# Half of the down product of an MLP as seven block products in place of eight, with the first sum of weight blocks on GpSimd

## The chip, the cores and the metric

One core of one Trainium2 chip runs the kernel. The metric is the device time of one execution in microseconds (us); the median of three runs of the kernel before is 2241.0 us (2240.79 to 2241.18). Engines are named as in the profile: PE multiplies matrices, DVE is VectorE, ACT is ScalarE, POOL is GpSimd, SP issues the DMAs.

## The reference

A decoder trunk of two layers on 256 tokens of 2048 features in float32. Each layer is a mixer (attention of several kinds) and then a dense MLP with a hidden width of 8192; a last norm follows. The part that matters here:

```python
def squared_relu_mlp(h, w1, w2):
    return jnp.square(jax.nn.relu(h @ w1)) @ w2

for layer in range(DEPTH):
    x = x + mixer(rmsnorm(x, ln_mix[layer]))
    x = x + squared_relu_mlp(rmsnorm(x, ln_mlp[layer]), mlp_w1[layer], mlp_w2[layer])
return rmsnorm(x, ln_final)
```

`h @ w1` is called the up product, the product with `w2` the down product.

## The kernel before

Weights are read once. `Weights.load` (L144) fetches four row tiles of 128 x 512 (1 MB) into one of three `raw` buffers. `Weights.get` (L154) takes two row tiles at a time and splits them into two halves of 12 bits that add up exactly: ACT casts `raw` to `wh` (L162), DVE subtracts `wh` from `raw` and gets `wl` (L163); there are three buffers of 1024 elements for each half. Activations are split in the same way, so a product of two float32 matrices is three passes (`mm`, L166 to L172: high x high, high x low, low x high), and PE reads float32 in the pass type fp32r.

An MLP works through its 8192 hidden features in four chunks of 2048 (`mlp`, L719). `up(c)` (L729) computes a chunk with the features on partitions, in four blocks of 512 features: `FeatGemm` (L211) makes two matmuls for each row tile and tile of features, one of 512 columns and one of 256 (L226, L227). ACT copies the four accumulators out (L740), DVE adds, squares (L741, L742) and both split the result into `hh` and `hl` (L743, L744). `down(c, h)` (L750) multiplies a chunk by 2048 rows of `w2`, in four blocks of 512 output columns, by `TokenGemm` (L182): for each row tile of weights and each of the two tiles of tokens three matmuls of 512 columns (L170 to L172). `add` (L747) puts the result, times the norm's factor, on the residual x. The order is up(0), up(1), down(0), up(2), down(1) and so on, so that a down product never follows its own up product. Accumulators come from six PSUM banks in turn (`bank`, L176); the last two of the eight are `ptr`'s.

In the mixers, products of the same kinds run (`heads`, `gemm_tok`), and small parts of attention wait in the list `pend`; `tick` (L109) slips one between the steps of a product.

Nobody writes the order of instructions on an engine by hand: a scheduler that estimates times while the program is built sets it, and on the chip each engine follows its queue in that order, as do the DMAs on SP's queue.

## Time and profile before

| what | us |
|---|---|
| median of three runs | 2241.0 |
| span of the profiled execution, first to last instruction | 2239.9 |
| PE busy | 2224.8 |
| DVE busy | 1318.0 |
| ACT busy | 1036.4 |
| POOL busy | 0.2 |

The profile gives one execution, whose span is 1.1 us under the median of the runs; the rest of this text counts in that span. A PE that is busy 99% of the time is one in which a matmul is always under way; whether it goes at its pace is read from the starts of successive matmuls, since their ends overlap.

### The profile page before, as it was taken

The numbers are of one execution on the slowest core, as the hardware profiler recorded it, in microseconds if no ns is written. First come the engines' busy times: TensorE is split into PE (matmuls) and PEld (weight loads), VectorE is DVE, ScalarE is ACT, GpSimd is POOL, SyncE is SP. The second block draws the span as 40 slices with busy tenths as digits, with TensorE's granted clock in tenths as the row PEclk, the third lists the DMA queues.
The fourth block names the chain that finished last, engine by engine and source line by source line (L and its number), as shares of the span: only waits on it lengthen the run. The fifth ranks groups of instructions, "written<-read, shape, count | busy, mean of one in ns | idle before, by whom it ended". The sixth has DMA issues, their size and how long they took to land.

```text
span 2239.9 us, 29663 instructions
## 1 busy us (share of the span) xinstructions
PE 2224.8 (99%) x12126; PEld 1913.7 (85%) x12126; DVE 1318.0 (59%) x1771; ACT 1036.4 (46%) x1369; POOL 0.2 (0%) x4
## 2 busy tenths in 40 slices
PE   8999999999999999999999999999999999999998
PEld 7899988888888888888899999888888888888887
DVE  6767665565545545655575666556565555465555
ACT  5444545555434434534444443455454344344333
POOL 0000000000000000000000000000000000000000
PEclk9999999999999999999999999999999999999999
DMA  7554545555555555555555555556555555555553
GB/s 244 177 164 148 170 137 172 183 187 187 188 188 189 188 188 190 188 188 186 188 171 170 177 164 170 173 180 204 190 181 192 189 191 188 188 187 190 188 188 132
DMA packets 207605, 406.65 MB, mean 182 GB/s; under 512 B 8614, under 2 KB 15468, under 8 KB 207340
## 3 DMA queue, kind: packets, MB, share of 16 engines
q1 hardware_dynamic: 207468, 404.75, 55.5%
q8 instruction: 95, 1.56, 0.3%
q14 instruction: 42, 0.34, 0.0%
HBM read 402.62 MB, written 2.10 MB: 181 GB/s over the span
## 4 chain that ended last, share of the span: by engine, by line
PE 99%; DMA 0%; DVE 0%; ACT 0%; SPq 0%; issue 0%; DVEq 0%
PE acc L226 21%; PE acc L172 21%; PE acc L171 21%; PE acc L170 21%; PE acc L227 11%; PE pt L236 1%; PE ps L458 1%; PE po L391 1%; PE pp L236 0%; PE po L392 0%; DMA raw<-in_e_w_in_dram 0%; PE ps L689 0%; PE ps L688 0%; DMA raw<-in_mlp_w_dram 0%; PE pi L170 0%; PE pi L171 0%
## 5 line engine op out<-in xcount | busy, mean ns | idle before, releaser
L163 DVE TENSOR_TENSOR wl<-raw,wh 128x1024 fp32r<-128x1024 f32 (+3 forms) x765 | 927.6, 1213 | 849.0 <-ACT wh L162 843.1
L162 ACT CAST wh<-raw 128x1024 fp32r<-128x1024 f32 (+3 forms) x765 | 794.5, 1039 | 1081.3 <-PE acc L172 572.1
L226 PE MATMUL acc<-xx,wh 128*128 128x512 f32 x2048 | 703.6, 395 | 0.0
L227 PE MATMUL acc<-xx,wl 128*128 128x256 f32 x2048 | 544.1, 281 | 0.0
L226 PEld LDWEIGHTS acc<-xx,wh 128*128 128x128 f32 x2048 | 378.2, 188 | 77.9
L172 PE MATMUL acc<-wh,hl 128*128 128x512 f32 (+1 forms) x1024 | 402.2, 393 | 0.0
L171 PE MATMUL acc<-wl,hh 128*128 128x512 f32 (+1 forms) x1024 | 400.0, 391 | 0.0
L227 PEld LDWEIGHTS acc<-xx,wl 128*128 128x128 f32 x2048 | 385.5, 188 | 12.5
L170 PE MATMUL acc<-wh,hh 128*128 128x512 f32 (+1 forms) x1024 | 361.0, 391 | 0.0
L171 PEld LDWEIGHTS acc<-wl,hh 128*128 128x128 f32 x1024 | 192.2, 188 | 45.8
L170 PEld LDWEIGHTS acc<-wh,hh 128*128 128x128 f32 x1024 | 191.7, 188 | 45.2
L172 PEld LDWEIGHTS acc<-wh,hl 128*128 128x128 f32 x1024 | 192.3, 188 | 44.2
L171 PE MATMUL acc<-xx,wh 128*128 128x256 f32 x768 | 216.5, 282 | 0.0
L170 PE MATMUL acc<-xx,wh 128*128 128x256 f32 x768 | 216.4, 282 | 0.0
L172 PE MATMUL acc<-xx,wl 128*128 128x256 f32 x768 | 215.5, 282 | 0.0
L171 PEld LDWEIGHTS acc<-xx,wh 128*128 128x128 f32 x768 | 144.7, 188 | 0.4
L170 PEld LDWEIGHTS acc<-xx,wh 128*128 128x128 f32 x768 | 144.7, 188 | 0.4
L172 PEld LDWEIGHTS acc<-xx,wl 128*128 128x128 f32 x768 | 144.3, 188 | 0.0
L171 PE MATMUL acc<-wl,xx 128*128 128x512 f32 (+1 forms) x320 | 127.5, 399 | 0.0
L172 PE MATMUL acc<-wh,xx 128*128 128x512 f32 (+1 forms) x320 | 125.5, 393 | 0.0
L170 PE MATMUL acc<-wh,xx 128*128 128x512 f32 (+1 forms) x320 | 119.7, 400 | 0.5 <-ACT xx L270 0.5
L171 PE MATMUL acc<-wl,oh 128*128 128x512 f32 x256 | 102.2, 399 | 0.0
(166 smaller groups left out, 1615.8 us busy)
## 6 DMA issues: line engine op xcount, KB each, us to landing
raw<-in_mlp_w_dram SPq DMA_DIRECT2D x252, 1024.0 KB, 5.1
raw<-in_o_w_in_dram SPq DMA_DIRECT2D x48, 1024.0 KB, 5.1
raw<-in_e_w_in_dram SPq DMA_DIRECT2D x35, 1024.0 KB, 5.1
raw<-in_e_w_out_dram SPq DMA_DIRECT2D x16, 1024.0 KB, 5.0
raw<-in_o_w_out_dram SPq DMA_DIRECT2D x16, 1024.0 KB, 5.1
raw<-in_mlp_w_dram SPq DMA_DIRECT2D x8, 512.0 KB, 3.8
raw<-in_e_w_uq_dram SPq DMA_DIRECT2D x4, 768.0 KB, 4.4
raw<-in_e_w_in_dram SPq DMA_DIRECT2D x4, 640.0 KB, 4.1
```

The lines of the kernel that those rows point to most:

```text
L162: nc.scalar.copy(hi, raw)
L163: nc.vector.tensor_tensor(lo, raw, hi.bitcast(F32), op=ALU.subtract)
L170: nc.tensor.matmul(o, ah, bh, start=first, stop=False, **kw)
L171: nc.tensor.matmul(o, ah, bl, start=False, stop=False, **kw)
L172: nc.tensor.matmul(o, al, bh, start=False, stop=last, **kw)
L226: nc.tensor.matmul(self.o[f], wh[:, kk, fs], xx[:, k], start=k == 0, stop=False, skip_group_check=True)
L227: nc.tensor.matmul(self.o[f][:, 0, :], wl[:, kk, fs], xx[:, k, 0], start=False, stop=k == KT - 1, skip_group_check=True)
L236: nc.tensor.transpose(o, src, ident[: src.shape[0], : src.shape[0]])
L391: nc.tensor.matmul(po[0][:, h % 2, :], values(h, 0), pr[h][:, :S], start=True, stop=False)
L458: nc.tensor.matmul(o, q[:, h, t * P : t * P + P], k[:, h, : SPAN[t][1]], start=True, stop=True)
```

## The change

Each down product of a chunk is done by halves. Column blocks 2 and 3 of 512 remain plain products (`plain`). Blocks 0 and 1 become products of 2 x 2 blocks with seven multiplications in place of eight (`SevenGemm`): a pair of row tiles of weights and 512 columns make four weight blocks of 128 x 256, two tiles of features and two of tokens four blocks of activations, and sums of the blocks are multiplied, seven products of three passes for each pair. The seven accumulate over the eight pairs in four PSUM banks, and `result` puts them together once.

The weights' sums are made for each pair: one addition of 512 elements on GpSimd (L250), two of 256 on DVE (L251, L252); then ACT and DVE split 1792 elements. The activations' sums are made once for each block of 512 hidden features, on DVE, behind the squared relu (`combine`, L281 to L283), in a buffer of the kind that raw weights use.

What goes with it: the order is up(0), down(0), up(1), down(1); in a down product four plain steps come first, then seven-steps and plain steps in turn, four seven-steps last. Weights are now split four row tiles at a time, in buffers of 2048 elements: in the MLPs three of `raw`, `wh` and `wl` each (one of them in the MLP's own pool, `more`), elsewhere two. Up blocks take the four `acc` banks and the other four in turn. Constants are loaded for each mixer, and the last norm's gains in four pieces.

```diff
         def get(self, k, n):
...
+            if halves is None:
+                halves = [h.rearrange("p (k n) -> p k n", n=self.width) for h in half_tiles(m * self.width)]
+                split(*halves, raw)
...
+    def in_turn(tag, dt, n):
+        if more and next(turns[tag]) % 3 == 2:
+            return more[0].tile([P, 2048], dt, name=nm(tag), tag=tag, bufs=1)[:, :n]
+        return wpool.tile([P, 2048], dt, name=nm(tag), tag=tag, bufs=2)[:, :n]
...
+    def split(hi, lo, raw):
+        nc.scalar.copy(hi, raw)
+        nc.vector.tensor_tensor(lo, raw, hi.bitcast(F32), op=ALU.subtract)
...
+    class SevenGemm:
+        PRODUCTS = ((0, 0, 1, 1), (0, 1, 6, 6), (1, 0, 4, 5), (1, 1, 5, 4), (2, 0, 2, 7), (2, 1, 7, 2), (3, 0, 3, 3))
...
+        def step(self, i):
+            raw = raw_tile(2048)
+            b = raw.rearrange("p (s n) -> p s n", n=256)
+            nc.sync.dma_start(raw[:, :1024].rearrange("p (k n) -> p k n", n=512),
+                              self.src[2 * i * P : (2 * i + 2) * P, :].rearrange("(k p) n -> p k n", p=P))
+            nc.gpsimd.tensor_add(b[:, 4:6], b[:, 1:3], b[:, 0:1].to_broadcast([P, 2, 256]))
+            nc.vector.tensor_add(b[:, 6], b[:, 4], b[:, 2])
+            nc.vector.tensor_add(b[:, 7], b[:, 6], b[:, 3])
+            halves = half_tiles(2048)
+            split(*(h[:, 256:] for h in halves), raw[:, 256:])
+            bh, bl = (h.rearrange("p (s n) -> p s n", n=256) for h in halves)
+            if self.o is None:
+                self.o = [bank((P, 2, 256)) for _ in range(4)]
+            for q, j, sa, sb in self.PRODUCTS:
+                mm(self.o[q][:, j, :], self.act(i, sa), (bh[:, sb], bl[:, sb]), i == 0 and j == 0, i == self.steps - 1,
+                   skip_group_check=True)
+
+        def result(self):
+            (p1, p6), (p7, p5), (p4, p3), (p2, _) = ((o[:, 0, :], o[:, 1, :]) for o in self.o)
...
+            nc.scalar.copy(c1, p1)
+            nc.vector.tensor_tensor(u2, p6, c1, op=ALU.subtract)
+            nc.vector.tensor_add(v[:, :, :256], self.o[1], u2.unsqueeze(1).to_broadcast([P, 2, 256]))
+            nc.vector.tensor_tensor(v[:, 0, 256:], p4, u3, op=ALU.subtract)
+            nc.vector.tensor_add(u3, p5, u3)
+            nc.vector.tensor_add(u4, p3, u4)
+            nc.vector.tensor_add(u2, p2, c1)
+            return [v[:, t, :] for t in range(NT)]
+
+    def combine(s):
+        n = s.shape[1]
+        nc.vector.tensor_tensor(s[:, :, 4:6, :], s[:, :, 0:1, :].to_broadcast([P, n, 2, 128]), s[:, :, 1:3, :], op=ALU.subtract)
+        nc.vector.tensor_tensor(s[:, :, 6, :], s[:, :, 1, :], s[:, :, 5, :], op=ALU.subtract)
+        nc.vector.tensor_tensor(s[:, :, 7, :], s[:, :, 3, :], s[:, :, 6, :], op=ALU.subtract)
...
             def up(c):
...
+                    o = FeatGemm(w1[:, c0 : c0 + 512], [psc, psc, ptr, ptr] if n % 2 else [acc] * 4).run()
+                    sums = raw_tile(2048).rearrange("p (k s n) -> p k s n", s=8, n=128)
...
+                            nc.scalar.copy(half[:, i], o[2 * j + i][:, 1, :])
+                            nc.vector.tensor_add(a[:, i], o[2 * j + i][:, 0, :], half[:, i])
                         nc.vector.scalar_tensor_tensor(a, a, 0.0, a, op0=ALU.max, op1=ALU.mult)
...
+                    combine(sums)
+                    split(*halves, sums)
...
             def down(c, act):
...
+                one, two = chained(plain(2), plain(3)), chained(seven(0), seven(1))
+                for _ in range(4):
+                    next(one)
+                left = [two, one]
+                while left:
+                    for g in list(left):
+                        if next(g, 0) == 0:
+                            left.remove(g)
...
+            down(0, act)
             for c in range(1, NCH):
-                cur = up(c)
-                down(c - 1, prev)
-                prev = cur
-            down(NCH - 1, prev)
+                down(c, up(c))
```

Three places show how the order on the engines moves. The first is DVE between two up blocks of the first MLP. Before, at the end of the second chunk's first block (`wl` is a low half of weights, `a` and `hl` belong to the block that PE has just finished):

```order
L163 TENSOR_TENSOR wl_4055<-raw_4052,wh_4054 128x1024
L163 TENSOR_TENSOR wl_4075<-raw_4052,wh_4074 128x1024
L741 TENSOR_TENSOR a_4033<-both_4032 128x512
L742 SCALAR_TENSOR_TENSOR a_4033<-a_4033 128x512
L163 TENSOR_TENSOR wl_4097<-raw_4094,wh_4096 128x1024
L741 TENSOR_TENSOR a_4041<-both_4040 128x512
L744 TENSOR_TENSOR hl_3841<-a_4033,hh_3840 128x512
L742 SCALAR_TENSOR_TENSOR a_4041<-a_4041 128x512
L163 TENSOR_TENSOR wl_4117<-raw_4094,wh_4116 128x1024
```

With the change, at the end of the second up block of the first chunk (`raw_3947` holds that block's sums, `wl_3974` is the next block's first weight set, `wl_4012` its second):

```order
L191 TENSOR_TENSOR wl_4012<-raw_4009,wh_4011 128x2048
L825 TENSOR_TENSOR raw_3947<-bank_3791,half_3950 128x256
L825 TENSOR_TENSOR raw_3947<-bank_3792,half_3950 128x256
L826 SCALAR_TENSOR_TENSOR raw_3947<-raw_3947 128x512
L825 TENSOR_TENSOR raw_3947<-bank_3793,half_3956 128x256
L825 TENSOR_TENSOR raw_3947<-bank_3794,half_3956 128x256
L826 SCALAR_TENSOR_TENSOR raw_3947<-raw_3947 128x512
L281 TENSOR_TENSOR raw_3947<-raw_3947 128x2x256
L282 TENSOR_TENSOR raw_3947<-raw_3947 128x2x128
L283 TENSOR_TENSOR raw_3947<-raw_3947 128x2x128
L191 TENSOR_TENSOR wl_3974<-raw_3971,wh_3973 128x2048
L191 TENSOR_TENSOR al_3949<-raw_3947,ah_3948 128x2048
```

Before, the work on a finished block lies between the subtractions of weights; now it is one run of nine instructions, with the next block's first weight set behind it.

The second place is DVE in the middle of a down product with the change (L251 and L252 make the last two sums of a seven-step's weights, `raw_4709` is a plain set):

```order
L251 TENSOR_TENSOR raw_4637<-raw_4637 128x256
L252 TENSOR_TENSOR raw_4637<-raw_4637 128x256
L251 TENSOR_TENSOR raw_4679<-raw_4679 128x256
L252 TENSOR_TENSOR raw_4679<-raw_4679 128x256
L191 TENSOR_TENSOR wl_4643<-raw_4637,wh_4642 128x1792
L191 TENSOR_TENSOR wl_4685<-raw_4679,wh_4684 128x1792
L191 TENSOR_TENSOR wl_4712<-raw_4709,wh_4711 128x2048
```

This is the pattern of two rounds: seven instructions where there were four subtractions of 1024 before, and the sums of the second seven-step stand ahead of the first one's subtraction.

The third place is DVE from the first down product to the next up product (`raw_5056` is the last seven-step, `raw_5101` and on are the up product's sets, L269 to L274 empty the accumulators of the last seven product):

```order
L191 TENSOR_TENSOR wl_5062<-raw_5056,wh_5061 128x1792
L191 TENSOR_TENSOR wl_5104<-raw_5101,wh_5103 128x2048
L191 TENSOR_TENSOR wl_5142<-raw_5139,wh_5141 128x2048
L269 TENSOR_TENSOR v_5087<-bank_4789,c_720_5086 128x256
L270 TENSOR_TENSOR v_5087<-bank_4790,v_5087 128x2x256
L271 TENSOR_TENSOR v_5087<-bank_4791,v_5087 128x256
L273 TENSOR_TENSOR v_5087<-bank_4791,v_5087 128x256
L274 TENSOR_TENSOR v_5087<-bank_4792,c_720_5086 128x256
L191 TENSOR_TENSOR wl_5180<-raw_5177,wh_5179 128x2048
L272 TENSOR_TENSOR v_5087<-bank_4790,v_5087 128x256
```

Two subtractions of the next up product's weights stand ahead of the first instruction that frees a bank, and a third ahead of L272.

## Rows read from the trace of the kernel before

**Rows 1.** The page: busy us of engines, share of the span, number of instructions.
```profile
PE 2224.8 (99%) x12126; PEld 1913.7 (85%) x12126; DVE 1318.0 (59%) x1771; ACT 1036.4 (46%) x1369; POOL 0.2 (0%) x4
```

**Rows 2.** Both MLPs: stretch, busy PE, PEld, DVE, ACT, POOL, granted clock, DMA, GB/s.
```profile
400.00:1117.00 717.00, 717.00 (x3604) 602.05 (x3603) 401.21 (x414) 329.60 (x383) 0.00 (x0) 1.00 0.58 187
...
1513.00:2230.00 717.00, 716.86 (x3681) 605.92 (x3680) 402.86 (x433) 325.20 (x383) 0.00 (x0) 1.00 0.57 185
```

**Rows 3.** PE in order of time, a step of a down product; columns start, duration.
```profile
1000.60 0.62 PE L170 MATMUL acc<-wh,hh 128*128 128x512 f32 x2
...
1003.40 0.62 PE L170 MATMUL acc<-wh,hh 128*128 128x512 f32 x2
```

**Rows 4.** PE in order of time, matmuls of 256 columns in the odd mixer.
```profile
1299.77 0.28 PE L171 MATMUL acc<-xx,wh 128*128 128x256 f32 x1
...
1301.89 0.28 PE L171 MATMUL acc<-xx,wh 128*128 128x256 f32 x1
```

**Rows 5.** Who waited for whom, us in total, times, longest.
```profile
DVE wl L163 <- ACT wh L162: 843.1, 681, 3.1
ACT wh L162 <- PE acc L172: 572.1, 350, 3.1
...
SPq L150 <- DVE wl L163: 1850.5, 350, 10.9
```

**Rows 6.** ACT and DVE in order of time, the same down product as rows 3.
```profile
1000.80 1.05 ACT L162 CAST wh<-raw 128x1024 fp32r<-128x1024 f32 x1 [1.75 <-PE acc L172]
...
999.08 1.22 DVE L163 TENSOR_TENSOR wl<-raw,wh 128x1024 fp32r<-128x1024 f32 x1 [1.58 <-ACT wh L162]
```

**Rows 7.** Groups of instructions by form: busy us, mean ns of one, idle before.
```profile
L163 DVE TENSOR_TENSOR wl<-raw,wh 128x1024 fp32r<-128x1024 f32 x739 | 905.1, 1225 | 826.9 <-ACT wh L162 821.3 <-PE pp L236 4.8
L162 ACT CAST wh<-raw 128x1024 fp32r<-128x1024 f32 x739 | 774.8, 1049 | 1049.7 <-PE acc L172 544.8 <-PE acc L226 331.2 <-PE acc L171 147.4
...
L740 ACT COPY both<-acc 128x512 f32<-128x512 f32 x128 | 74.2, 584 | 3.6
...
L743 ACT CAST hh<-a 128x512 fp32r<-128x512 f32 x64 | 39.6, 618 | 0.7
...
L163 DVE TENSOR_TENSOR wl<-raw,wh 128x512 fp32r<-128x512 f32 x10 | 6.9, 690 | 8.1 <-ACT wh L162 8.1
```

**Rows 8.** DMA issues: count, KB each, median us from issue to landing.
```profile
raw<-in_mlp_w_dram SPq DMA_DIRECT2D x252, 1024.0 KB, 5.1
raw<-in_o_w_in_dram SPq DMA_DIRECT2D x48, 1024.0 KB, 5.1
raw<-in_e_w_in_dram SPq DMA_DIRECT2D x35, 1024.0 KB, 5.1
raw<-in_e_w_out_dram SPq DMA_DIRECT2D x16, 1024.0 KB, 5.0
raw<-in_o_w_out_dram SPq DMA_DIRECT2D x16, 1024.0 KB, 5.1
raw<-in_mlp_w_dram SPq DMA_DIRECT2D x8, 512.0 KB, 3.8
```

**Rows 9.** ACT and DVE in order of time, a stretch of the even mixer.
```profile
103.59 1.05 ACT L162 CAST wh<-raw 128x1024 fp32r<-128x1024 f32 x1 [1.88 <-PE acc L172]
...
105.21 1.22 DVE L163 TENSOR_TENSOR wl<-raw,wh 128x1024 fp32r<-128x1024 f32 x1
```

**Rows 10.** Busy times near the start (columns as in rows 2).
```profile
8.00:13.00 5.00, 4.49 (x11) 3.04 (x10) 1.75 (x4) 3.88 (x11) 0.00 (x0) 1.00 1.03 374
```

**Rows 11.** PE in order of time, the start of the program.
```profile
8.32 1.05 PE L171 MATMUL acc<-wl,xx 128*128 128x512 f32 x2
9.18 1.05 PE L172 MATMUL acc<-wh,xx 128*128 128x512 f32 x2
...
15.62 0.40 PE L171 MATMUL acc<-wl,xx 128*128 128x512 f32 x1
15.86 0.39 PE L172 MATMUL acc<-wh,xx 128*128 128x512 f32 x1
```

More of the change, by code (lines that the diff above doesn't have):

```diff
@@ L211, in decoder_trunk, with __init__ @@
     class FeatGemm:
-        def __init__(self, src, wide=False):
+        def __init__(self, src, of):
             self.w = Weights([src], KT)
-            self.o = [bank((P, 2, S), wide) for _ in range(4)]
+            self.o = [bank((P, 2, S), f) for f in of]
             self.steps = KT // 2
@@ L488, in load_gains @@
     def load_gains(at, gs):
-        rows = wpool.tile([P, P], F32, name=nm("rows"), tag="ra", bufs=1)
+        rows = mix[-1].tile([P, P], F32, name=nm("rows"), tag="ra", bufs=1)
         n = 0
@@ L754, in down, with plain, seven, chained @@
                     blocks[3:] = [slice(1536, 1792)]
-                for n, cs in enumerate(blocks):
-                    o = gemm_tok(h, 16, [w2[c * 2048 : (c + 1) * 2048, cs]], wide=True)
+                src = lambda cs: w2[c * 2048 : (c + 1) * 2048, cs]
+                def plain(n):
+                    cs = blocks[n]
+                    g = TokenGemm(row, 16, [src(cs)], psc)
+                    for i in range(8):
+                        g.step(i)
+                        tick()
+                        yield
                     for t in range(NT):
-                        add(t, cs, o[t][:, : cs.stop - cs.start])
+                        add(t, cs, g.o[t][:, : cs.stop - cs.start])
                     if last:
                         done(n, cs)
+                def seven(n):
+                    cs = blocks[n]
+                    g = SevenGemm(pool, slot, 8, src(cs))
+                    for i in range(8):
+                        g.step(i)
+                        tick()
+                        yield
+                    for t, v in enumerate(g.result()):
+                        add(t, cs, v)
+                    if last:
+                        done(n, cs)
+                def chained(*gs):
+                    for g in gs:
+                        yield from g
+                one, two = chained(plain(2), plain(3)), chained(seven(0), seven(1))
[6 more added lines that the diff above has]
+                            left.remove(g)
                 if last and tail:
                     cs = slice(1792, 2048)
-                    wh, wl = halves()
-                    wts = Weights([w2[c * 2048 : (c + 1) * 2048, cs]], 16)
-                    for k in range(0, 16, 2):
-                        wts.get(k, 2, (wh[:, k : k + 2, :], wl[:, k : k + 2, :]))
-                    hh, hl = h
+                    wts = Weights([w2[c * 2048 : (c + 1) * 2048, cs]], 16, [(0, 8), (8, 8)])
+                    ws = [wts.get(k, 8) for k in range(0, 16, 8)]
                     for t in range(NT):
```

145 lines of the change are left out of this document (85 added, 60 removed).

## The prediction

> **What bounds the kernel now.** I read the busy shares first, then the busy times by stage, then single stretches. PE is busy 99% of the span [rows 1], and in both MLP stages for the whole of 717 us, the others far less [rows 2]. A busy matrix engine can still be badly fed, so the pace was read too: in a down product matmuls of 512 columns start every 0.2333 us (from 1000.60 to 1003.40 are twelve of them: 2.80 us for two row tiles of weights) [rows 3], and where a product moves 256 columns they start every 0.118 us (18 in 2.12 us) [rows 4]. Both paces are even, so PE waits for nothing. Who waits is on the other side: DVE's subtraction waits for ACT's cast, 843.1 us in all, the cast for PE to give buffers back, 572.1 us behind L172 alone, and the DMA queue for the subtraction, 1850.5 us [rows 5]. In a down step the cast takes 1.05 us and sits idle 1.75, the subtraction 1.22 and 1.58 [rows 6]. So less PE work is worth its full time only while this chain (load, cast, subtraction, matmul) stays ahead of PE. The change shortens PE and lengthens the chain.
>
> **Prices.** The cast takes 1.049 us for 1024 elements and 0.618 for 512, the subtraction 1.225 and 0.690 [rows 7]; along these lines (estimates) a cast of 2048 takes 1.91 and of 1792 1.70, a subtraction of 2048 2.30, of 1792 2.03, an addition of 256 0.42. A load of 1 MB lands in 5.1 us, of 512 KB in 3.8 [rows 8]. GpSimd's addition of 512 is not in the trace (its four instructions take 0.2 us in all [rows 1]). DVE's 0.690 for 512 is the low end, twice DVE's time for 1024, 2.45, the high one; I take 1.2, DVE's row for 1024, as if two inputs were read in turn. The Trainium skill (GPSIMD Engine Reference, section 3.1) gives 4.5 us for a GpSimd addition of 2048 and twice DVE's time; an estimate from that page is 1.1 us, which would leave the sum as it is; no run here shows it.
>
> **The sum**, from the profiled span 2239.9 us; the median of the runs is 2241.0, 1.1 more.
>
> 1. PE work. A seven-product step is 21 matmuls of 256 columns, 21 x 0.118 = 2.48 us, in place of 2.80. There are 8 down products x 2 column blocks x 8 steps = 128: **-41 us**, all on the path.
>
> 2. Up products. The sums now take one of the three raw buffers, and DVE builds all slots behind PE's last matmul of the block: ACT's copy (about 0.4; 0.584 for 512 [rows 7]), an addition 0.42, the square and L281 0.69 each, L282 and L283 0.42 each, with 0.2 until the matmul has ended (PE begins the next step at 1000.60, the cast that waits for the one before it at 1000.80 [rows 3, 6]): 3.25 us, before the next subtraction in the queue. The order shows what stands behind it. In one block of each up product it is the next block's *first* weight set: ready at 3.25 + 2.30 = 5.55 us where PE wants it at 0. Four matmuls that need only the cast (0.93) are ahead of it, so PE loses 4.6 or more. In the two other blocks it is the set that frees a buffer for the *third* set: load 5.55 to 10.7, cast to 12.6, subtraction to 14.9; PE wants it at 11.2 (two sets of 5.6), and has again 0.93 of other work: 2.8. Per up product 4.6 + 2 x 2.8 = 10.2, eight of them: **+82**. The first block of each has no sums in front.
>
> 3. Down products. *Start:* the first seven-step takes its raw buffer from the same place: free at 5.55, load to 9.35, GpSimd 10.6, L251 and L252 11.4, those of the second step 13.7 (the order puts them first), subtraction 15.75; PE has finished its four plain steps at 11.2. With 0.9 of other work it loses 3.6 in this order; the other two orders that the scheduler made (third and second raw buffer free first) give 6.3 and 2: 4 on average. *Middle:* two rounds need PE 2 x (2.48 + 2.80) = 10.56 us. A raw buffer of a seven-step is taken for 3.8 + 1.2 + 0.84 + 1.70 + 2.03 = 9.6, so 1 us is left for queueing, with DVE busy 2 x 2.87 + 2.30 = 8.0 of it. Where the order gives PE only one seven-step (2.48) between two plain sets, the second set's cast and subtraction (4.2) can't fit; following the orders through, I get 1.4 to 6 us, and take 4. *End:* the last four or five steps are seven-steps alone. Three buffers of 9.6 give one step in 3.2 us against PE's 2.48, and the order makes some wait twice: 3 to 9, I take 5. Together 13 x 8: **+104**.
>
> 4. Down to up. The next up block needs the accumulators of the last seven product. DVE reaches L269 only behind the second up set, whose buffer was freed by the last step but one: load 5.1, cast 1.91, subtraction 2.30 make 9.3, while PE ends 2.03 + 0.42 + 1.7 + 2.0 = 6.2 after that same point: 3.1 to 3.6 lost, and about 1.5 more until L272 frees the second bank behind the next subtraction. Five us, at six such places and at the end of the first MLP: **+35**.
>
> 5. Mixers (115 loads of 1 MB [rows 8], outside the MLPs): two raw buffers and sets cast whole in place of 3 and half sets. A set given back is ready 0.2 + 1.91 + 2.30 = 4.4 later and wanted after 5.6. Subtractions behind other DVE work start late (0.57 in the stretch shown, where the cast ended at 104.64 [rows 9]); late by more than 1.1 they now stop PE. From 0 (none is) to 30; I take **+10**. Constants, gains and moved scratch tiles: 0, since they are a few small loads and the same DVE instructions; if they come late, one load (5.1).
>
> Sum -41 + 82 + 104 + 35 + 10 = +190: span 2430, and with the 1.1 a time of **2431 us**.
>
> The DMA bytes stay as they were (187 GB/s in an MLP [rows 2]; 374 near the start show room [rows 10]).
>
> **Rivals.**
> *The port.* GpSimd and DVE might not read at the same time. The Trainium skill (SBUF — State Buffer, section "Who interferes with whom") says that a DVE instruction with two SBUF inputs and a GpSimd instruction that reads SBUF exclude each other; no run here shows it yet. As a mechanism: DVE has 8.0 of 10.56 us taken, and 2 x 1.2 more make 10.4, so each queueing counts. 128 additions x 1.2 = 154 us if all of it reaches PE, 77 if half does: **2508**. Against it: GpSimd often runs where DVE waits for it anyway. Chance 0.2.
> *The pace of PE.* The first matmuls start 0.43 us apart (two in the 0.86 from 8.32 to 9.18), from 15.62 on 0.24, while the granted clock is shown at 1.00, its 2.4 GHz level [rows 10, 11]. If PE falls back to that pace after waits of 3 to 5 us, about 40 places lose some 2 us each: **2511**. Chance 0.1.
> *Half the waits.* If orders bite less (loads land sooner, subtractions slip in), half of the 231 us of waits remain: 2241 - 41 + 115 = **2315**. Chance 0.14.
> *Not slower.* The third set of each up block is the place: DVE and ACT idle for 1.58 and 1.75 of 2.80 us now [rows 6], so the chain may catch up between blocks. It decides at 41 / 8 = 5.1 us of waiting per pair of up and down product. With 10 us in the mixers left: **2210**. Against it: the start of the down product and the accumulators together cost more than that by two separate chains. Chance 0.06.
>
> **Numbers.** The forecast has 0.50. The range takes half the waits at its low end and the port at its high one, with 30 us each for the prices' ends: 2300 to 2540; below it and above it about 0.1 each. A measurement here can tell 0.2% (4.5 us). Faster 0.05, same 0.01, slower 0.94.
>
> **What would show it.** PE busy at 88 to 92% of the span, with idle time before matmuls at L307, L198 and L197 that ends on DVE's wl at L191 and on L269 and L272; steps of 2.48 us at L197 to L199 with 256 columns; the stretch from one up product to the next at 190 to 210 us, where it is 179.2 now (717 / 4 [rows 2]); mixers within 30 us of now. It would be wrong if the MLP stages took under 717 us, if PE idled mostly in the mixers, or if GpSimd's additions took over 2.45 us.

## The result and the profile after

The changed kernel takes **2639.1 us** (median of four runs, 2637.3 to 2642.4) against 2241.1 (2240.8 to 2241.3) beside it: a ratio of 1.178, with a 95% interval of 1.176 to 1.180. The forecast was 2431 us with a range of 2300 to 2540: the direction was right, the size far too small. The profiled execution has a span of 2637.1 us, 397.2 more than before.

The page of the changed kernel, busy times (as [rows 1]) and granted clock in 40 slices:

```profile
PE 2336.3 (89%) x13278; PEld 2031.0 (77%) x13278; DVE 1622.5 (62%) x1928; ACT 1060.1 (40%) x1030; POOL 208.6 (8%) x132
...
PEclk9999999899889899989999999998998999898988
```

PE has 301 us without a matmul, where there were 15. What the busy line doesn't tell stands in the second row: the clock was at full speed throughout the MLPs before and now dips in both of them. The two MLP stages (columns as in [rows 2]) show it as 0.93 and 0.91; they take 893 and 915 us where they took 720.4 and 718.7 from the first up matmul to the last down matmul:

```profile
408.50:1301.50 893.00, 765.54 (x4193) 654.68 (x4191) 556.48 (x551) 352.40 (x279) 106.28 (x64) 0.93 0.44 150
1713.50:2628.50 915.00, 777.07 (x4256) 669.58 (x4256) 562.93 (x567) 346.09 (x268) 102.08 (x64) 0.91 0.43 145
```

The groups by form, busy time, mean and idle time ahead (as [rows 7]):

```profile
L307 PE MATMUL bank<-xx,wh 128*128 128x512 f32 x2048 | 753.1, 415 | 95.6 <-ACT wh L190 76.7 <-DVE v L269 18.9
...
L308 PE MATMUL bank<-xx,wl 128*128 128x256 f32 x2048 | 580.3, 295 | 39.0 <-DVE wl L191 38.8
...
L198 PE MATMUL bank<-wl,ah 128*128 128x256 f32 x960 | 279.4, 303 | 52.6 <-DVE wl L191 52.0
...
L190 ACT CAST wh<-raw 128x1792 fp32r<-128x1792 f32 x128 | 214.5, 1691 | 400.8 <-DVE raw L252 343.4 <-PE bank L199 47.7 <-issue 7.6
L250 POOL TENSOR_TENSOR raw<-raw 128x512 f32<-128x512 f32 x128 | 208.4, 1630 | 2395.4 <-DMA raw<-in_mlp_w_dram 1551.3 <-DVE raw L282 808.5 <-DVE x L833 13.4
...
L251 DVE TENSOR_TENSOR raw<-raw 128x256 f32<-128x256 f32 x128 | 63.7, 498 | 154.4 <-POOL raw L250 154.4
```

PE now waits for the cast (127 us in all) and the subtraction (125 us), and the cast of a seven-step for the sums (343.4 us). The same from the list of waits (as [rows 5]), and the loads (as [rows 8]):

```profile
PE bank L198 <- DVE wl L191: 85.9, 60, 5.5
PE bank L197 <- ACT wh L190: 50.2, 31, 5.0
...
DVE wl L191 <- ACT wh L190: 685.0, 235, 8.8
ACT wh L190 <- DMA raw<-in_mlp_w_dram: 404.3, 92, 8.1
ACT wh L190 <- DVE raw L252: 343.4, 82, 9.7
ACT wh L190 <- PE bank L199: 195.9, 69, 10.3
```

```profile
raw<-in_mlp_w_dram SPq DMA_DIRECT2D x190, 1024.0 KB, 5.2
raw<-in_mlp_w_dram SPq DMA_DIRECT2D x132, 512.0 KB, 3.6
```

Before, the cast waited for PE to give buffers back; now it waits first for loads and for the sums, and the loads are no slower than they were: they are asked for late. At full clock a seven-step goes at the pace that was forecast, 0.119 us from start to start (ten steps between these two rows; [rows 4] gave 0.118):

```profile
800.06 0.28 PE L199 MATMUL bank<-wh,al 128*128 128x256 f32 x1
...
801.25 0.28 PE L199 MATMUL bank<-wh,al 128*128 128x256 f32 x1
```

**Where the time went.** I took the start of every matmul in the trace and compared the time to the next start with the full pace (0.2333 us for 512 columns, 0.118 for 256). An excess of over 0.3 us is a wait, put down to its place; a smaller one is the clock's where the granted clock is 0.50, else a small lag. This gives, against the terms of the forecast:

| step of the forecast | forecast | measured |
|---|---|---|
| 1 PE's work | -41 | -42 |
| 2 up products (third sets 60, first sets 46, other 18) | +82 | +124 |
| 3 down products: start, middle, end | 32 + 32 + 40 | 44 + 77 + 33 |
| 4 down to up (six places 22, end of the first MLP 4.5) | +35 | +27 |
| 5 mixers (even 8, odd 17, behind the last MLP -1) | +10 | +24 |
| half clock in the MLPs | 0 | +88 |
| small lags in the MLPs | 0 | +23 |
| sum | +190 | +398 |

The line between middle and end is a matter of choice: the end is counted here from the 14th seven-step of a down product. Counted from the 13th, where the four seven-steps start that stand alone, the middle is 64 us and the end 46.

**A wait, and the clock behind it.** PE in order of time in an up product of the first MLP:

```profile
465.50 0.58 PE L308 MATMUL bank<-xx,wl 128*128 128x256 f32 x1 [4.12 <-DVE wl L191]
465.88 0.63 PE L307 MATMUL bank<-xx,wh 128*128 128x512 f32 x1
466.31 0.63 PE L308 MATMUL bank<-xx,wl 128*128 128x256 f32 x2
...
469.06 0.40 PE L307 MATMUL bank<-xx,wh 128*128 128x512 f32 x1
469.29 0.28 PE L308 MATMUL bank<-xx,wl 128*128 128x256 f32 x1
```

From 465.88 to 466.31 a matmul of 512 columns takes 0.43 us; from 469.06 to 469.29 it takes 0.23. The stretches around it (granted clock is the third number from the end):

```profile
455.00:462.10 7.10, 4.12 (x21) 2.95 (x20) 5.48 (x8) 4.58 (x6) 0.00 (x0) 1.00 0.21 80
462.20:469.00 6.80, 3.50 (x12) 3.11 (x13) 5.38 (x5) 1.90 (x1) 0.00 (x0) 0.50 0.34 100
469.00:475.80 6.80, 6.80 (x41) 5.95 (x40) 2.29 (x1) 3.79 (x2) 0.00 (x0) 1.00 0.56 211
```

PE was busy for 4.12 of 7.10 us, then the clock stood at 0.50, the 1.2 GHz level, for 6.8 us, in which half the time was another wait and the other half went at half pace. The two MLPs have 46 such intervals, 285 us in all, and lose 88 us of work time in them.

**The place that the forecast had right.** DVE between two up blocks, with the chain that was written down beforehand:

```profile
654.93 0.75 DVE L825 TENSOR_TENSOR raw<-bank,half 128x256 f32<-128x256 f32 x2
...
659.02 0.43 DVE L283 TENSOR_TENSOR raw<-raw 128x256 f32<-128x256 f32 x1
659.36 2.28 DVE L191 TENSOR_TENSOR wl<-raw,wh 128x2048 fp32r<-128x2048 f32 x1
```

```profile
658.38 1.20 PE L307 MATMUL bank<-xx,wh 128*128 128x512 f32 x4 [2.26 <-ACT wh L190]
661.70 0.58 PE L308 MATMUL bank<-xx,wl 128*128 128x256 f32 x1 [2.12 <-DVE wl L191]
```

PE waits 2.26 us for the cast and 2.12 for this subtraction; 4.6 were forecast, all of it on the subtraction.

**The place that it had too cheap.** In another chunk a third set is late. DVE, then PE:

```profile
886.43 2.29 DVE L191 TENSOR_TENSOR wl<-raw,wh 128x2048 fp32r<-128x2048 f32 x1 [1.86 <-ACT wh L190]
888.64 2.29 DVE L191 TENSOR_TENSOR al<-raw,ah 128x2048 fp32r<-128x2048 f32 x1
898.15 2.29 DVE L191 TENSOR_TENSOR wl<-raw,wh 128x2048 fp32r<-128x2048 f32 x1 [7.23 <-ACT wh L190]
```

```profile
898.17 2.07 PE L307 MATMUL bank<-xx,wh 128*128 128x512 f32 x4 [7.95 <-ACT wh L190]
```

The raw buffer that the set needs is the sums' own. It comes free only when the sums are split, at 890.93; that stands behind a weight subtraction which itself had to wait. Then come the load, the cast and the subtraction: 8 us late in place of 2.8. The list of waits of the DMA queue (as [rows 5]) has 20 loads that waited for such a split:

```profile
SPq L158 <- DVE al L191: 157.6, 20, 16.9
```

**GpSimd and DVE.** DVE and GpSimd in a down product:

```profile
547.86 2.03 DVE L191 TENSOR_TENSOR wl<-raw,wh 128x1792 fp32r<-128x1792 f32 x1 [1.89 <-ACT wh L190]
551.06 0.42 DVE L251 TENSOR_TENSOR raw<-raw 128x256 f32<-128x256 f32 x1 [1.17 <-POOL raw L250]
...
553.61 1.51 DVE L252 TENSOR_TENSOR raw<-raw 128x256 f32<-128x256 f32 x1
555.04 0.41 DVE L251 TENSOR_TENSOR raw<-raw 128x256 f32<-128x256 f32 x1
```

```profile
548.15 2.87 POOL L250 TENSOR_TENSOR raw<-raw 128x512 f32<-128x512 f32 x1 [3.10 <-DMA raw<-in_mlp_w_dram]
553.53 1.30 POOL L250 TENSOR_TENSOR raw<-raw 128x512 f32<-128x512 f32 x1 [2.50 <-DMA raw<-in_mlp_w_dram]
```

An addition on GpSimd takes 1.29 us when DVE is idle (mean of the 40 such ones). The one that started under DVE's subtraction took 2.87, and ended 1.13 after it; DVE's addition of 256, otherwise 0.42, took 1.51 when it started 0.08 after GpSimd's. In these rows one waits for the other to finish, both ways. It depends on where the inputs lie: L833, which reads one of its two large inputs from PSUM, takes 0.74 us beside an addition on GpSimd (8 times) as without one (22 times).

### The profile page after: what moved, and what is told of

It reads as the page before. It is cut to its first block, busy times and chain, and to the rows that moved or that the text cites. A ratio compares the mean times of both kernels' runs of the same rounds, so it can differ in the third digit from the quotient of the medians.

```text
span 2637.1 us, 31930 instructions
## 1 busy us (share of the span) xinstructions
PE 2336.3 (89%) x13278; PEld 2031.0 (77%) x13278; DVE 1622.5 (62%) x1928; ACT 1060.1 (40%) x1030; POOL 208.6 (8%) x132
## 4 chain that ended last, share of the span: by engine, by line
PE 23%; DVE 16%; DMA 13%; ACT 5%; POOL 3%; issue 2%; POOLq 0%; ACTq 0%; SPq 0%; DVEq 0%
DMA raw<-in_mlp_w_dram 13%; DVE wl L191 10%; PE bank L198 5%; PE bank L199 5%; PE bank L197 5%; ACT wh L190 4%; PE bank L307 4%; POOL raw L250 3%; PE bank L308 2%; DVE al L191 1%; DVE raw L251 1%; DVE raw L826 1%; DVE raw L252 1%; DVE raw L825 1%; ACT ah L190 1%
## 5 line engine op out<-in xcount | busy, mean ns | idle before, releaser
L191 DVE TENSOR_TENSOR wl<-raw,wh 128x2048 fp32r<-128x2048 f32 (+3 forms) x450 | 985.4, 2202 | 699.7 <-ACT wh L190 685.0
L190 ACT CAST wh<-raw 128x2048 fp32r<-128x2048 f32 (+3 forms) x450 | 813.9, 1822 | 1255.4 <-DMA raw<-in_mlp_w_dram 404.3
L307 PE MATMUL bank<-xx,wh 128*128 128x512 f32 x2048 | 753.1, 415 | 95.6 <-ACT wh L190 76.7
L308 PE MATMUL bank<-xx,wl 128*128 128x256 f32 x2048 | 580.3, 295 | 39.0 <-DVE wl L191 38.8
L198 PE MATMUL bank<-wl,ah 128*128 128x512 f32 (+1 forms) x1440 | 476.9, 339 | 83.3 <-DVE wl L191 82.5
L307 PEld LDWEIGHTS bank<-xx,wh 128*128 128x128 f32 x2048 | 402.7, 199 | 189.9 <-ACT wh L190 85.1
L197 PE MATMUL bank<-wh,ah 128*128 128x512 f32 (+1 forms) x1440 | 422.1, 335 | 53.9 <-ACT wh L190 49.3
L199 PE MATMUL bank<-wh,al 128*128 128x512 f32 (+1 forms) x1440 | 467.7, 333 | 0.0
L308 PEld LDWEIGHTS bank<-xx,wl 128*128 128x128 f32 x2048 | 412.2, 201 | 65.5 <-DVE wl L191 55.5
L250 POOL TENSOR_TENSOR raw<-raw 128x512 f32<-128x512 f32 x128 | 208.4, 1630 | 2395.4 <-DMA raw<-in_mlp_w_dram 1551.3
L197 PE MATMUL bank<-xx,wh 128*128 128x256 f32 x768 | 217.3, 285 | 6.3 <-DVE v L269 4.3
L198 PE MATMUL bank<-xx,wh 128*128 128x256 f32 x768 | 217.2, 284 | 1.2 <-DVE xx L352 1.2
L199 PE MATMUL bank<-xx,wl 128*128 128x256 f32 x768 | 214.4, 285 | 0.0
L251 DVE TENSOR_TENSOR raw<-raw 128x256 f32<-128x256 f32 x128 | 63.7, 498 | 154.4 <-POOL raw L250 154.4
L197 PEld LDWEIGHTS bank<-xx,wh 128*128 128x128 f32 x768 | 146.5, 191 | 7.1 <-DVE v L269 4.5
L198 PEld LDWEIGHTS bank<-xx,wh 128*128 128x128 f32 x768 | 147.0, 191 | 1.7 <-DVE xx L352 1.4
L199 PEld LDWEIGHTS bank<-xx,wl 128*128 128x128 f32 x768 | 144.7, 191 | 0.2
```

What stands on the lines that cost most here:

```text
L190: nc.scalar.copy(hi, raw)
L191: nc.vector.tensor_tensor(lo, raw, hi.bitcast(F32), op=ALU.subtract)
L197: nc.tensor.matmul(o, ah, bh, start=first, stop=False, **kw)
L198: nc.tensor.matmul(o, ah, bl, start=False, stop=False, **kw)
L199: nc.tensor.matmul(o, al, bh, start=False, stop=last, **kw)
L250: nc.gpsimd.tensor_add(b[:, 4:6], b[:, 1:3], b[:, 0:1].to_broadcast([P, 2, 256]))
```

## The experiments

Sixteen runs, each against the kernel before on the same chip. The expectations used a first count of the waits that put parts of the mixers and of other places into the middle of the down products (96 us, and 165 for the down products); the table above has 77 and 153.

### One: the first sum on DVE

```diff
-            nc.gpsimd.tensor_add(b[:, 4:6], b[:, 1:3], b[:, 0:1].to_broadcast([P, 2, 256]))
+            nc.vector.tensor_add(b[:, 4:6], b[:, 1:3], b[:, 0:1].to_broadcast([P, 2, 256]))
```

> The changed kernel with one word altered: the first sum of weight blocks (L250) runs on DVE in place of GpSimd. Theory A (waits come from the chain load, sums, cast, subtraction, and from buffers and the order of DVE's queue; the clock falls behind the waits): the sum takes about 0.7 us on DVE in place of 1.29 to 2.9 on GpSimd, so the chain of a seven-product step is 0.6 to 1 us shorter, but DVE has 128 x 0.7 = 90 us more to do. PE's waits in the middle of the down products (96 us) fall by a quarter to a half, some more in clock: 2590 us (2560 to 2620). Theory B (GpSimd's pace and its exclusion with DVE make most of the waits in down products): these waits fall by 80 us and the clock's loss by 25: 2530 or less. Theory C (DVE's own work is the limit): slower than the changed kernel, 2650 or more.

2633.3 us (2629.2 to 2636.6), ratio 1.175 (1.173 to 1.177): 6 us less, none of the three. Waits in the MLPs 284 us (changed kernel: 305), loss to half clock 105 (88). GpSimd's pace is not what holds the changed kernel.

### Two: four raw buffers

```diff
     def raw_tile(n):
-        return in_turn("raw", F32, n)
+        if more and next(turns["raw"]) % 2:
+            return more[0].tile([P, 2048], F32, name=nm("raw"), tag="raw", bufs=2)[:, :n]
+        return wpool.tile([P, 2048], F32, name=nm("raw"), tag="raw", bufs=2)[:, :n]
```

> The changed kernel with four buffers of raw weights in the MLPs in place of three, taken in turn (room is made by one buffer of the last gains less). The seven products, GpSimd's sums and the loop order stay. Theory A: in an up product the sums of activations no longer cost the weights a buffer (the waits before the third set, 60 us, go for the most part), and in a down product a raw buffer's cycle of about 10.1 us stands against four buffers in place of three, so waits at the start and in the middle of down products (132 us) halve; with a third of the saved waits again in clock: 2639 - 60 - 65 - 40 = 2475 us (2420 to 2550). Theory B (GpSimd): only the up products gain, 2560 to 2580. Theory D (the order of DVE's queue, not the count of buffers): 2600 or more.

**2400.4 us** (2395.4 to 2406.3), ratio 1.071 (1.069 to 1.073): 239 us less, more than any theory said. An up product and the down product behind it, columns as above:

```profile
615.50:708.00 92.50, 92.15 (x512) 79.46 (x512) 57.17 (x53) 37.29 (x32) 1.64 (x1) 0.98 0.49 165
708.00:812.90 104.90, 91.67 (x530) 80.30 (x529) 80.70 (x79) 48.43 (x30) 22.24 (x16) 0.95 0.52 176
```

The up products are nearly without waits (12 us where there were 124), though DVE still builds the sums between two blocks. So in the up products that order costs nothing when a set more lies ready: what they lacked was a buffer, since the sums hold one of three. The start of down products falls from 44 to 12 us, their middle only from 77 to 69. The clock gives back 47.

### Three: casts in halves

```diff
-                split(*halves, raw)
+                for c in (slice(0, m // 2), slice(m // 2, m)) if m % 2 == 0 else [slice(0, m)]:
+                    split(*(h[:, c, :] for h in halves), raw[:, c, :])
```

> The changed kernel with the cast and the subtraction of a plain set of weights done in two halves, as before the change, in the same buffers of 2048; seven-product steps stay whole. Theory A: the first half of a set is ready after 1.05 + 1.23 us in place of 1.91 + 2.29, so the waits before first sets of up blocks (46 us) shrink by half and those of plain sets in down products by a third, while each pair of halves costs ACT and DVE about 0.3 us more in all: 2580 us (2530 to 2620). Theory E (casting whole sets is the main cause): 2500 or less. Theory D (the order of DVE's queue): within 30 us of 2639, to either side, since the scheduler only places other pieces behind the same work.

2551.6 us (2547.1 to 2553.8), ratio 1.138 (1.137 to 1.140), near the first theory's 2580, though not by its parts: first sets fell by 4 us only (46 to 42), third sets from 60 to 38, the middle of down products stayed (79), and the even mixer came back from 408.5 to 402.7 us.

### Four: no seven products

```diff
-                one, two = chained(plain(2), plain(3)), chained(seven(0), seven(1))
+                one, two = chained(plain(2), plain(3)), chained(plain(0), plain(1))
...
-                    combine(sums)
-                    split(*halves, sums)
+                    split(*(h[:, :, 0:4, :] for h in halves), sums[:, :, 0:4, :])
```

> The changed kernel with all four column blocks of a down product plain, so without seven products, without GpSimd, without sums of weights or activations (activations are split as they are); buffers, whole-set casts, loop order and constants stay as in the changed kernel, and the result is still the reference's. Theory A (the sums lengthen the chain): PE's work is 41 us more, the waits of down products (165 us) and between products (28) go, those of up products (124) shrink by a third, the clock's loss of 92 goes down to about 30: 2639 + 41 - 165 - 28 - 41 - 62 = 2385 us (2320 to 2450). Theory F (the restructuring costs nothing, all is the seven products): 2241 + 17 in the mixers = 2258 or less than 2290. Theory E (whole-set casts and buffers cost it all): 2550 or more.

2351.3 us (2350.5 to 2353.7), ratio 1.050 (1.048 to 1.051). That is in the first theory's range. So 110 us of the loss come with the buffers and the order, without a single sum of blocks (the activations still hold a raw buffer until they are split), and 288 more with the seven products and their sums. Here the down products wait 10 us in all, the up products 67.

### Five to eight: the middle of the down products

The fifth run has the edits of two and three together. The sixth is two with

```diff
-                        if next(g, 0) == 0:
+                        if [next(g, 0) for _ in range(2)][1] == 0:
```

and the eighth all three of these, with the up blocks' banks exchanged from the second chunk on:

```diff
-                    o = FeatGemm(w1[:, c0 : c0 + 512], [psc, psc, ptr, ptr] if n % 2 else [acc] * 4).run()
+                    o = FeatGemm(w1[:, c0 : c0 + 512], [psc, psc, ptr, ptr] if (n + (c > 0)) % 2 else [acc] * 4).run()
```

> Four raw buffers as in the second run, and plain sets cast and subtracted in two halves as in the third. Theory G (half buffers in a down product: the three pairs of wh and wl serve a seven-step, a plain set and a seven-step in turn, so each keeps its role; the plain set's pair is held over both of its steps with a seven-step between, and its successor's cast and subtraction, 1.91 + 2.29 us, must fit into one seven-step of 2.48): with halves 1.05 + 1.23 fit, so the waits in the middle of down products fall from 80 to about 25 us, the clock gives back another 15 and the mixers 6: 2320 us (2290 to 2350). Theory B or D (GpSimd and its sums, or the order of DVE's queue, hold the middle of down products): 2370 or more.

2341.9 us (2340.7 to 2346.5), ratio 1.046 (1.044 to 1.047).

> Four raw buffers as in the second run, whole casts, and the turns in a down product taken two steps at a time: two seven-steps, then both steps of one plain set, in place of one and one. Theory G: the plain set's successor now has two seven-steps, 4.96 us, for its 4.2 us of cast and subtraction, so the middle of down products loses 80 - 50 and the clock 15 less: 2335 us (2300 to 2370). Theory B or D: two seven-steps in a row want their sums at once, and the time stays at 2400 or rises.

2391.0 us (2388.0 to 2394.5), ratio 1.067 (1.065 to 1.069).

> The changed kernel with four raw buffers, halves of plain sets, two steps at a time in down products, and, from the second chunk of an MLP on, the up blocks starting on the other four accumulator banks, so that the first one needn't wait for the last seven product to be put together. Theories A and G and the account of the waits between down and up (20 us): PE work as in the changed kernel, mixers 10 us over before; of the waits some 40 stay (starts and ends of down products), with 12 in clock: 2241 - 41 + 10 + 40 + 12 = 2262 us (2225 to 2310). Were the waits to move only to the next resource (DVE's queue): 2320 or more.

2319.8 us (2313.7 to 2321.7), ratio 1.035 (1.033 to 1.036): not the 2262 of the first account but the value of the second, that the waits move to the next resource. The theory of half buffers (G) falls, though the fifth run's time lies in its range: the middle of the down products still waits 66 us in the fifth run, 72 in the sixth and 58 in the eighth; what the fifth gained lies elsewhere (up products, starts and ends of down products, the even mixer, and the clock). In the eighth the up products wait nowhere, and between down and up next to nothing is left of 22. Its down product, by stretch:

```profile
682.50:779.90 97.40, 90.11 (x535) 78.33 (x534) 87.24 (x87) 47.16 (x38) 24.86 (x15) 0.98 0.54 182
```

DVE is busy 87 of 97 us, more than PE's 84.8 us of work there. That made the next theory. (Over the eight down products DVE is busy 80 to 90 us; in two it has clearly less than PE, 80 us, and these took 96 us all the same.)

The seventh run tests the clock: spare matmuls in the up products of the changed kernel.

```diff
+            if self.busy.get(i):
+                o = self.o[0] if i == 0 else bank((P, 2, S), self.other)
+                for j in range(self.busy[i]):
+                    nc.tensor.matmul(o, xx[:, j % KT, 0, :P], xx[:, j % KT], start=True, stop=True, skip_group_check=True)
```

> The changed kernel with spare matmuls of 512 columns (their results are overwritten or never read) in the up products, 9 to 28 at a place, 365 in all or 85 us at full pace, meant for the places where PE waited there. Nothing else is altered. Theory H (the granted clock falls because PE stood idle before): where spare matmuls fill a wait, no low interval follows, the stretch that follows runs at 0.233 us per 512 columns, and the stages are shorter by some 1.7 us at each such place; with all in place 2639 - 40 = 2600 us; spare work beside its place costs its own length, at most 45 us in all, so 2590 to 2680. Theory I (the clock falls for another reason, such as DMA or the other engines' load): as many low intervals in the up products as before, and 2640 to 2720.

2637.4 us (2629.5 to 2642.6), ratio 1.177 (1.174 to 1.179). That time lies in theory H's range and 3 us below theory I's, so it decides little. The trace does: in the up products 13 low intervals start and the clock is low for 88 us in all, where the changed kernel has 24 and 150 us, while their length is the same (899 and 903 us) and the down products, without spare work, stay as they were (low for 141 and 135 us). The up products' waits fall from 124 to 65 us and their loss to half clock from 46 to 30; the spare work itself takes up what that saves. Clock and work of PE go together; the busy times of DVE and ACT are those of the changed kernel to within 1 us.

### Nine to twelve: is DVE the bound?

All four are the eighth run with one edit: the sums of weight blocks left out; one column block as seven products; the first sum on DVE (the diff of run one); all blocks plain (the diff of run four).

```diff
-            nc.gpsimd.tensor_add(b[:, 4:6], b[:, 1:3], b[:, 0:1].to_broadcast([P, 2, 256]))
-            nc.vector.tensor_add(b[:, 6], b[:, 4], b[:, 2])
-            nc.vector.tensor_add(b[:, 7], b[:, 6], b[:, 3])
...
-            split(*(h[:, 256:] for h in halves), raw[:, 256:])
+            split(*(h[:, :1024] for h in halves), raw[:, :1024])
```

> The kernel of the eighth run with the sums of weight blocks left out (L250 to L252 of the changed kernel), so that 1024 elements are cast and subtracted for a seven-step in place of 1792; the same number of matmuls reads the four unsummed blocks. It leaves out that part of the computation. Theory J (with buffers enough, DVE is the bound in the down products: it is busy 83 to 90% of them in the eighth run, and GpSimd shuts it out for some more): DVE has 16 x 1.6 = 26 us less to do per down product, which then takes PE's 84.6 us in place of 97: 2320 - 8 x 12 = 2224 us (2205 to 2245). Theory K (buffers or their order still hold it): 2280 or more.

2214.2 us (2213.7 to 2214.5), ratio 0.988 (0.986 to 0.990). A down product:

```profile
670.00:754.80 84.80, 84.80 (x530) 76.24 (x529) 51.59 (x54) 37.19 (x38) 0.00 (x0) 1.00 0.64 216
```

PE never waits, DVE has 52 us of 85. This is what PE's part of the change is worth. Leaving the sums out takes away DVE's work and the longer chain of a seven-step together, so this run does not tell the two apart.

> The kernel of the eighth run with one column block of a down product as seven products in place of two. Theory J: PE has 21 us more to do over the whole, DVE 13 us less per down product (73 us of the 87 that PE needs), so most of the waits go: 2320 - 8 x (97 - 90) = 2264 us (2240 to 2290). Theory K: the waits halve at most with the number of seven-steps, and PE's 21 us come on top: 2290 to 2310.

2291.9 us (2288.7 to 2294.5), ratio 1.023 (1.021 to 1.024): the second theory's value. Of the waits left (46 us) some 25 stand 13 to 17 us into each down product, where the fourteenth run below still has its 25; the others are spread over the rest, most of them among the seven-steps.

> The kernel of the eighth run with the first sum of weight blocks on DVE in place of GpSimd. Theory L (where DVE is the bound, GpSimd's sum costs DVE more than it saves, since the two don't run at the same time: the sum holds DVE off for up to 1.29 us, and DVE would need 0.69 itself): faster by 8 x 16 x 0.3 to 0.6, so 2240 to 2285 us. Theory M (the sum on GpSimd is off DVE's back): 8 x 16 x 0.69 = 88 us more on the bound engine, 2370 to 2410.

2292.1 us (2289.9 to 2295.6), ratio 1.023 (1.021 to 1.025), 28 us less than the eighth: the sign of theory L, at half its size. The busy times of DVE in the eighth run and in this one:

```profile
PE 2232.3 (96%) x13278; PEld 1967.4 (85%) x13278; DVE 1673.7 (72%) x2248; ACT 1091.6 (47%) x1350; POOL 224.2 (10%) x132
...
PE 2216.3 (97%) x13278; PEld 1957.0 (85%) x13278; DVE 1676.5 (73%) x2376; ACT 1090.2 (48%) x1350; POOL 0.2 (0%) x4
```

DVE makes 128 more sums, 88 us of work at 0.69, and is busy 3 us longer: in the eighth run GpSimd's sums had made DVE's other instructions longer by 75 us. So GpSimd's help gave DVE next to nothing. Why the kernel is 28 us faster without it is not shown in parts; the chain of a seven-step is also shorter with the sum on DVE.

> The kernel of the eighth run with all column blocks of the down products plain, as in the fourth run: no seven products and no sums. Theories A and J: PE's work is that of the kernel before, four buffers leave no waits in up or down products, and some 10 us in the mixers stay: 2255 us (2245 to 2275). If the structure (loop order, buffers of whole sets, constants loaded in parts) costs something that the buffers didn't cure: 2290 or more.

2248.5 us (2247.5 to 2249.5), ratio 1.003 (1.002 to 1.005). With four buffers and halves the structure costs 8 us, in the mixers alone. From here to the ninth run are 34 us, the seven products without the sums of weights; with them, to the eighth, there are 71 in the other direction.

### Thirteen to sixteen: seven-steps spread out

One column block as seven products, one seven-step ahead of each whole plain set:

```diff
-                one, two = chained(plain(2), plain(3)), chained(seven(0), seven(1))
+                one, two = chained(plain(2), plain(3), plain(1)), chained(seven(0))
...
-                        if next(g, 0) == 0:
+                        if [next(g, 0) for _ in range(1 if g is two else 2)][-1] == 0:
```

> The kernel of the tenth run (four raw buffers, halves, one column block as seven products) with its eight seven-steps spread out, one before each whole plain set, and the first sum on DVE. Theory J (DVE is the bound where seven-steps stand close): in a round DVE needs 3.56 + 2.4 = 6.0 us of PE's 2.48 + 5.6 = 8.1, so no waits stay; the time of the twelfth run less half of the seven products' gain, 2248.5 - 20.5 = 2228 us, 2222 to 2240 with some waits left: just faster than the kernel before. Theory K (waits come with seven-steps however they stand): 2260 or more.

2265.6 us (2261.9 to 2266.9), ratio 1.011 (1.009 to 1.012). Theory J's 2228 is missed by 37 us. The number is that of theory K, but not by its mechanism: the 24 us of waits left do not come with each seven-step, nearly all of them stand 13 to 17 us into each down product.

> The same as the thirteenth run with the first sum left on GpSimd. Theory L (GpSimd and DVE shut each other out; with DVE busy for three quarters that costs little but the longer chain of a seven-step): 3 to 15 us more than the thirteenth run. Theory M (off DVE's back): the same or some us less than the thirteenth run, since DVE has 8 x 8 x 0.69 = 44 us less to do.

2262.7 us (2261.3 to 2269.8), ratio 1.011 (1.009 to 1.012). Spread out, the seven-steps cost 29 us less than close together (tenth run), and what is left is for the most part some 3 us of waits near the start of each down product. The two runs can't be told apart: with room on DVE, it does not matter who adds.

The fifteenth run gives the fourth buffer to the sums alone,

```diff
-                    sums = raw_tile(2048).rearrange("p (k s n) -> p k s n", s=8, n=128)
+                    sums = pool.tile([P, 2048], F32, name=nm("sums"), tag="sums", bufs=1).rearrange("p (k s n) -> p k s n", s=8, n=128)
```

and the sixteenth starts with `range(6)` plain steps in place of `range(4)`.

> The fourteenth run with the fourth buffer of raw weights given to the sums of activations alone, and the weights' three taken in turn. Theory N (what is left, 25 us of waits and 6 to 10 in clock, comes at the start of each down product, where the last block's sums hold a raw buffer until DVE has split them, so the second plain set is loaded late): these waits go, 2262.6 - 25 - 6 = 2232 us (2226 to 2245). Theory O (three buffers in turn are too few for a seven-step's cycle of 10.1 us even when spread): 2262 or more.

**2234.9 us** (2233.0 to 2235.9, seven runs), ratio 0.9973 (0.9961 to 0.9984): **faster than the kernel before**, by 5.6 us or 0.3%. Both MLPs:

```profile
404.60:1117.40 712.80, 712.80 (x3907) 614.67 (x3906) 504.13 (x570) 344.28 (x374) 50.90 (x32) 1.00 0.57 191
1509.40:2224.50 715.10, 712.02 (x3977) 617.37 (x3975) 506.39 (x585) 338.07 (x368) 53.79 (x32) 1.00 0.56 187
```

PE is busy for all but 3 us, at full clock; the two stages take 7.6 and 3.6 us less than before, and the mixers 5 us more. Of the 20.5 us that one block is worth to PE, 11 thus arrive; waits of 3.5 us and small lags of 6 take the rest.

> The fourteenth run (four raw buffers in turn, one of them taken by sums) with six plain steps ahead of the first seven-step in place of four. Theory N: the third plain set is on its way before the sums are split, and PE has 5.6 us more of plain work while DVE catches up: half of the waits at least go, 2240 to 2252 us. Theory O: no change, 2260 or more.

2241.5 us (2239.7 to 2246.0), ratio 1.0004 (0.9996 to 1.0013), no difference from before. Both runs speak for the same cause: the last block's sums held a raw buffer at the start of the down product.

## Why the prediction was right and wrong, point by point

- **What bounds it** was right: PE's work was full, the chain behind it had room, and the change shortened the one and lengthened the other. PE was busy 89% of the span, as forecast, and its idle time ended on the subtraction (125 us) and L269 (25), as forecast, but also on the cast (127), which the list of signs did not name. Two more signs came out otherwise: from one up product to the next it took 222 to 230 us, where 190 to 210 were named, and 18 of GpSimd's 128 additions took over 2.45 us, with a mean of 1.63.
- **Step 1** was right: -42 for -41 in the trace, and 34 us between the twelfth and the ninth run, on the chip.
- **Step 2** named both waits and the places (one first set and two late sets in most up products) but not all of the price. First sets: 46 for 8 x 4.6 = 37. Third sets: 60 for 45, since the buffer comes free with the split of the sums, not with the weight subtraction at 5.55 us. The cause is shown: with a buffer more these waits go.
- **Step 3**: start and end were near (44 for 32, 33 for 40). **The middle was the worst of the waits**: 77 for 32 (64 where the end is counted from the 13th seven-step). The text counted 8.0 of 10.56 us for DVE and left "1 us for queueing". It left out what GpSimd holds DVE off for (30 us of longer DVE instructions in all, from instructions that overlap an addition against those that don't) and the additions to the residual (L833). With buffers enough DVE is busy 80 to 90 of 96 to 105 us; without the sums and what they add to cast and subtraction, PE does not wait. In the changed kernel itself both limits hold together, and how the 77 us divide between them stays open.
- **Step 4** was too dear: 27 for 35, at its seven places.
- **Step 5** was too cheap: 24 for 10, towards the upper end of its bounds. Of the odd mixer's 17 us, 7 are a wait for the first set of the MLP behind it, and 4 are two waits at its start. With halves the even mixer takes 403 us, where it took 408.5: there whole casts were the cause; the rest of the odd one was not taken apart.
- **The step that failed** is that the waits of steps 2 to 4 were counted at full pace. "The pace of PE" stood among the rivals, with a chance of 0.1, as another way for it to go, and at 80 us. It was no other way: the 88 us come with the waits, since a stretch at half clock follows them. It does not take waits of 3 to 5 us either: in the tenth run nine of the ten low intervals follow waits of 2.5 us at most. The rows that showed the half pace were read ([rows 11]), with the granted clock beside them as 1.00 ([rows 10]). That reading was wrong: in the trace of the kernel before the clock's records begin at 15.1 us, and a stretch without a record is shown as 1.00. The pace changes at that record:

```profile
13.47 1.85 PE L236 MATMUL pt<-cst,x 128*128 128x128 f32 x8
15.03 0.75 PE L170 MATMUL acc<-wh,xx 128*128 128x512 f32 x2
```

  The first of these two matmuls of 512 columns takes 0.36 us from start to start, the second 0.23, where those ahead took 0.43. In the changed kernel (first record at 11.6 us) and in the ninth run (10.6) the pace changes at the first record too. So the half pace at the start was the price that the sum lacked.
- **The error of 208 us** is made up of the clock (88), the middle (45), third and first sets (24 of the 42 in step 2), the mixers (14) and small lags (23) for the most part. The low end of the range, 2300, is also 15 above its own rule (2315 less 30); nothing hangs on it.
- **The port** rival had its mechanism right and its price wrong. The Trainium skill (SBUF — State Buffer, section "Who interferes with whom") says that a DVE instruction with two SBUF inputs contends with a GpSimd instruction that reads SBUF, for a port pair that one of them holds alone; the trace agrees (2.87 and 1.51 us for 1.29 and 0.42). But moving the sum to DVE bought 6 us in the changed kernel, where DVE had idle time anyway, and 28 in the eighth run, where it was busy 83 to 90% of a down product; 77 had been given. These are prices of the move, which also shortens a chain and gives DVE 88 us of sums; the exclusion alone has no price of its own here.
- **Not slower** did not happen, though the sixteenth run comes to it and the fifteenth beyond it.

## What to carry to other kernels

Waits of a matrix engine cost more than their length: with 305 us of waits came 88 of half clock in the changed kernel, and over all the runs with more than 20 us of waits 11 to 39 us for each 100, so they are terms to be added, not rivals. A buffer lent to another purpose is a buffer less for the pipeline: count a ring's cycle with everyone who takes from it. Before a saving on the bound engine is booked, count the second engine's load in that stage alone (in the eighth run DVE was at 72% of the span and at 83 to 90% of a down product), and spread the steps that load it.

## What the runs showed of the hardware that was not expected

- The granted clock fell to 0.50 inside a program that had been at full speed for hundreds of microseconds, after a stretch in which PE was busy for 4.12 of 7.10 us; 512 columns then took 0.43 us in place of 0.23. Shorter waits were enough in the tenth run, where it fell ten times. With spare matmuls in the up products 13 such intervals started there in place of 24.
- An addition of 512 on GpSimd took 1.29 us alone and up to 3.1 beside DVE, and DVE's addition of 256 took 1.51 us in place of 0.42 beside GpSimd; an instruction of DVE that reads one large input from PSUM was not held up (0.74 us with and without). In the eighth run 128 such additions cost DVE 75 us and spared it 88.
